# Rotary embedding on one core: the tables are loaded first, the head of batch 0 behind them

## The chip, the cores and the metric

The kernel runs on one core of one Trainium2 chip. Its time is the device time of one execution in microseconds (us). Before the change the median of three runs is 316.88 us (316.84 to 317.36). The core has several engines with an instruction stream each; four of them do something here: VectorE (DVE) multiplies and adds, ScalarE (ACT) converts number formats, and GpSimd (POOL) and SyncE (SP) issue transfers. The transfers are carried out by the core's 16 DMA engines. On-chip memory has 128 partitions.

## The reference: what is computed

```
x1, x2 = x[..., :32], x[..., 32:]        # x: (8, 2048, 16, 64) float32
out1 = x1 * cos - x2 * sin               # cos, sin: (2048, 32) float32
out2 = x1 * sin + x2 * cos               # the same table row for all 8 batches and 16 heads
out  = concatenate([out1, out2], axis=-1)
```

Each batch is 8 MB (2048 x 16 x 64 float32), so 64 MB are read and 64 MB are written; the tables have 256 KB each. Per element there are two products and a sum.

## The kernel before

A batch's 2048 positions are split so that partition p has positions 16p to 16p+15 (J = 16 "rows" in each partition). One tile `xt` holds a whole batch in float16, 128 partitions x 16384 elements; `io_pool` has five such buffers (NBUF = 5). The conversions between float32 in the main memory and float16 on the chip are made in the transfers that GpSimd issues (q0 in the profile): `load` (line 52) and `store` (line 60) are such casting transfers, of one 64 KB row of the main memory for each partition.

All of GpSimd's transfers go through one ring and are worked off in the order in which they were issued. That order is: loads of batches 0 to 3; the first row of batch 0 as a store (line 100, `first`); load 4; the rest of batch 0; batch 1; load 5 (it waits until batch 0's stores have landed, because it takes its buffer); load 6 (waits for batch 1's store); stores 2 and 3; load 7 (waits for store 2); stores 4, 5 and 6; and batch 7 in two parts (lines 130 and 132).

At the start and at the end SyncE's queue (q1) helps, which moves data without a cast. At the start it brings the first two rows of each partition of batch 0 as float32 into the tile `head` (JA = 2, 1 MB, line 36), and ScalarE converts them into `xt` (line 84; line 52's first load leaves these rows out, so it has 14 rows). Behind the head SyncE issues the sine and the cosine table (lines 44 and 45). ScalarE makes three float16 operands of them: the sine, the negative sine (both in `sin_h`, lines 88 and 89) and the cosine (`cos_h`, line 90). At the end ScalarE converts the last two rows of batch 7 into `head` (line 140) and SyncE stores them (line 141) once the part of line 130 has landed.

`rotate` is VectorE's work on a batch: v = (swapped halves of xt) x sin_h (line 73), xt = xt x cos_h (line 79), xt = xt + v (line 81). It is called for the two head rows first, then for the other 14 of batch 0, and then once for each batch.

ScalarE's stream before the change is: activation table, head cast (line 84), the two sine casts, the cosine cast, and much later line 140. Each engine works its stream in order, so a wait holds everything behind it. In the changed file the lines are numbered otherwise: the tables' issues are 40 and 41, the head's is 42, the casts are 84 to 86 for the tables and 87 for the head. From the stores on the numbers are the same in both.

Of the kernel before, what the change touches and what calls it, by code (L numbers as in the profile page):

```python
# [1 line left out]

# [4 lines left out]


@with_exitstack  # L10
def kernel(
    ctx: ExitStack,
    tc: tile.TileContext,
    x: bass.AP,
    cos: bass.AP,
    sin: bass.AP,
    out: bass.AP,
):
    nc = tc.nc
    f16 = mybir.dt.float16  # L20
    f32 = mybir.dt.float32

    B, S, H, D = x.shape
    Dh = D // 2
    P = nc.NUM_PARTITIONS
    J = S // P
    NBUF = 5

    const_pool = ctx.enter_context(tc.tile_pool(name="rope_const", bufs=1))
    io_pool = ctx.enter_context(tc.tile_pool(name="rope_io", bufs=NBUF))  # L30
    tmp_pool = ctx.enter_context(tc.tile_pool(name="rope_tmp", bufs=1))

    JA = 2
    head = const_pool.tile([P, JA, H, D], f32)
    x0 = x[0].rearrange("(p j) h d -> p j (h d)", j=J)
    nc.sync.dma_start(  # L36
        out=head.rearrange("p j h d -> p (j h d)"),
        in_=x0[:, 0:JA, :].rearrange("p j f -> p (j f)"),
    )
    sin_f = const_pool.tile([P, J, Dh], f32)  # L40
    cos_f = const_pool.tile([P, J, Dh], f32)
    cos_h = const_pool.tile([P, J, Dh], f16)
    sin_h = const_pool.tile([P, J, D], f16)
    nc.sync.dma_start(out=sin_f, in_=sin.rearrange("(p j) d -> p j d", j=J))  # L44
    nc.sync.dma_start(out=cos_f, in_=cos.rearrange("(p j) d -> p j d", j=J))

    loads = []

    def load(b):
        xt = io_pool.tile([P, J, H, D], f16)  # L50
        j0 = JA if b == 0 else 0
        dma = nc.gpsimd.dma_start(  # L52
            out=xt[:, j0:J, :, :].rearrange("p j h d -> p (j h d)"),
            in_=x[b].rearrange("(p j) h d -> p j (h d)", j=J)[:, j0:J, :].rearrange("p j f -> p (j f)"),
        )
        loads.append(dma)
        return xt

    def store(b, xt, j0=0):
        return nc.gpsimd.dma_start(  # L60
            out=out[b].rearrange("(p j) h d -> p j (h d)", j=J)[:, j0:J, :].rearrange("p j f -> p (j f)"),
            in_=xt[:, j0:J, :, :].rearrange("p j h d -> p (j h d)"),
        )

    def rotate(xt, j0, j1):
        v = tmp_pool.tile([P, J, H, D], f16)
        n = j1 - j0
        js = slice(j0, j1)
        shape = [P, n, H, 2, Dh]
        sin_b = sin_h[:, js, :].rearrange("p j (e d) -> p j e d", e=2).unsqueeze(2).to_broadcast(shape)  # L70
        cos_b = cos_h[:, js, :].unsqueeze(2).to_broadcast([P, n, 2 * H, Dh])
        xe = xt[:, js, :, :].rearrange("p j h (e d) -> p j h e d", e=2)
        nc.vector.tensor_mul(  # L73
            out=v[:, js, :, :].rearrange("p j h (e d) -> p j h e d", e=2),
            in0=xe[:, :, :, ::-1, :],
            in1=sin_b,
        )
        xw = xt[:, js, :, :].rearrange("p j h (e d) -> p j (h e) d", d=Dh)
        nc.vector.tensor_mul(out=xw, in0=xw, in1=cos_b)  # L79
        xa = xt[:, js, :, :].rearrange("p j h d -> p (j h d)")  # L80
        nc.vector.tensor_add(out=xa, in0=xa, in1=v[:, js, :, :].rearrange("p j h d -> p (j h d)"))  # L81

    tiles = [load(b) for b in range(NBUF - 1)]
    nc.scalar.copy(  # L84
        out=tiles[0][:, 0:JA, :, :].rearrange("p j h d -> p (j h d)"),
        in_=head.rearrange("p j h d -> p (j h d)"),
    )
    nc.scalar.copy(out=sin_h[:, :, Dh:D], in_=sin_f)  # L88
    nc.scalar.mul(out=sin_h[:, :, 0:Dh], in_=sin_f, mul=-1.0)  # L89
    nc.scalar.copy(out=cos_h, in_=cos_f)  # L90
    rotate(tiles[0], 0, JA)
    def part(b, j0, j1):
        return (
            out[b].rearrange("(p j) h d -> p j (h d)", j=J)[:, j0:j1, :].rearrange("p j f -> p (j f)"),
            tiles[b][:, j0:j1, :, :].rearrange("p j h d -> p (j h d)"),
        )

    def store_rows(b, j0, j1):
        dst, src = part(b, j0, j1)
        return nc.gpsimd.dma_start(out=dst, in_=src)  # L100

    first = store_rows(0, 0, 1)
    tc.add_manual_dep(
        first.ins,
        loads[NBUF - 2].ins.name,
        mybir.DependencyInfo(mybir.DependencyClass.NoSync, mybir.DependencyReason.DATA),
        reason="order of the ring",
    )
    tiles.append(load(NBUF - 1))
    tc.add_manual_dep(  # L110
        loads[NBUF - 1].ins,
        first.ins.name,
        mybir.DependencyInfo(mybir.DependencyClass.NoSync, mybir.DependencyReason.DATA),
        reason="order of the ring",
    )
    for b in range(B):
        rotate(tiles[b], JA if b == 0 else 0, J)
        if b < B - 1:
            st = store(b, tiles[b], 1 if b == 0 else 0)
            if b == 0:  # L120
                tc.add_manual_dep(
                    st.ins,
                    first.ins.name,
                    mybir.DependencyInfo(mybir.DependencyClass.NoSync, mybir.DependencyReason.DATA),
                    reason="order of the ring",
                )
        if b + NBUF < B:
            tiles.append(load(b + NBUF))
    dst, src = part(B - 1, 0, 9)
    gate = nc.gpsimd.dma_start(out=dst, in_=src)  # L130
    dst, src = part(B - 1, 9, J - JA)
    rest = nc.gpsimd.dma_start(out=dst, in_=src)  # L132
    tc.add_manual_dep(
        rest.ins,
        gate.ins.name,
        mybir.DependencyInfo(mybir.DependencyClass.NoSync, mybir.DependencyReason.DATA),
        reason="order of the ring",
    )
    dst, src = part(B - 1, J - JA, J)
    nc.scalar.copy(out=head.rearrange("p j h d -> p (j h d)"), in_=src)  # L140
    end = nc.sync.dma_start(out=dst, in_=head.rearrange("p j h d -> p (j h d)"))
    tc.add_manual_dep(
        end.ins,
        gate.ins.name,
        mybir.DependencyInfo(mybir.DependencyClass.Sync, mybir.DependencyReason.DATA),
        reason="the last rows go out behind this part",
    )


# [1 line left out]
_INS = ['x', 'cos', 'sin']  # L151
_OUTS = [((8, 2048, 16, 64), 'float32')]


# [23 lines left out]
```

## Time and profile before

| what | us |
|---|---|
| median of 3 runs | 316.88 (316.84 to 317.36) |
| span of the profiled execution | 315.7 |
| VectorE busy | 209.1 |
| ScalarE busy | 6.8 |
| GpSimd busy (it issues transfers) | 9.9 |
| first product on VectorE starts / third of them ends | 15.86 / 36.78 |
| first store issued | 37.06 |
| load of batch 7 issued / landed | 199.17 / 237.44 |
| last store issued | 306.43 |

The profiled execution is one execution recorded by the hardware; its span runs from the first to the last instruction, and the page gives no other time of it. The time of a run has some 1.2 us around such a span. In the profile "x3" is a count, "L73" a line of the kernel, "v<-xt,sin_h" an operation by its operands, and an arrow in the list of waits says whom an engine waited for. Rows of the list of waits give the total, how many times, and the longest. A DMA share of 1.00 means that all 16 DMA engines had a packet under way all the time. The table of transfer issues gives the size and the median time from the issue to the landing. "Landing" is the moment when all parts of a transfer have been signalled.

### The profile page before, as it was taken

The numbers are of one execution on the slowest core, as the hardware profiler recorded it, in microseconds if no ns is written. First come the engines' busy times: TensorE is split into PE (matmuls) and PEld (weight loads), VectorE is DVE, ScalarE is ACT, GpSimd is POOL, SyncE is SP. The second block draws the span as 40 slices with busy tenths as digits, with TensorE's granted clock in tenths as the row PEclk, the third lists the DMA queues.
The fourth block names the chain that finished last, engine by engine and source line by source line (L and its number), as shares of the span: only waits on it lengthen the run. The fifth ranks groups of instructions, "written<-read, shape, count | busy, mean of one in ns | idle before, by whom it ended". The sixth has DMA issues, their size and how long they took to land.

```text
span 315.7 us, 122 instructions
## 1 busy us (share of the span) xinstructions
DVE 209.1 (66%) x27; ACT 6.8 (2%) x6; POOL 9.9 (3%) x22
## 2 busy tenths in 40 slices
DVE  0010699999999999999999999994009994000000
ACT  4100000000000000000000000000000002000000
POOL 3000100000000000001000000100000001000000
DMA  9899999999999989999999999999999999999998
GB/s 277 183 262 208 199 220 245 199 199 199 266 199 199 498 374 523 399 332 241 224 199 199 390 407 399 399 531 266 199 249 482 399 399 515 415 399 399 432 434 330
DMA packets 3168, 101.71 MB, mean 322 GB/s; under 512 B 352, under 2 KB 352, under 8 KB 736
## 3 DMA queue, kind: packets, MB, share of 16 engines
q0 software_dynamic: 2592, 99.09, 98.1%
q1 hardware_dynamic: 576, 2.62, 2.3%
HBM read 67.63 MB, written 67.11 MB: 427 GB/s over the span
## 4 chain that ended last, share of the span: by engine, by line
DVE 25%; DMA 22%; issue 18%; another core or an unknown queue 17%; POOL 1%; ACT 1%; SPq 0%; POOLq 0%; DVEq 0%; ACTq 0%
DMA xt<-in_x_dram 12%; DMA cos_f<-in_cos_dram 10%; DVE xt L79 8%; DVE xt L81 8%; DVE v L73 8%; ACT head L140 1%; POOL out_dram L60 1%; POOL xt L52 0%; ACT cos_h L90 0%; SPq L44 0%; SPq L36 0%; POOLq L52 0%; POOLq L60 0%; DVEq L73 0%
## 5 line engine op out<-in xcount | busy, mean ns | idle before, releaser
L73 DVE TENSOR_TENSOR v<-xt,sin_h 128x16384 f16<-128x16384 f16 (+2 forms) x9 | 69.7, 7744 | 36.8 <-DMA xt<-in_x_dram 20.7
L79 DVE TENSOR_TENSOR xt<-xt,cos_h 128x16384 f16<-128x16384 f16 (+2 forms) x9 | 69.7, 7744 | 17.5 <-ACT cos_h L90 17.2
L81 DVE TENSOR_TENSOR xt<-xt,v 128x16384 f16<-128x16384 f16 (+2 forms) x9 | 69.7, 7744 | 0.3
L52 POOL DMA_DIRECT2D xt<-in_x_dram x8 | 4.4, 557 | 111.1 <-DMA out_dram<-xt 110.3
L140 ACT CAST head<-xt 128x2048 f32<-128x2048 f16 x1 | 1.9, 1897 | 229.5 <-DVE xt L81 229.5
L60 POOL DMA_DIRECT2D out_dram<-xt x7 | 3.7, 535 | 63.9 <-DVE xt L81 63.9
L130 POOL DMA_DIRECT2D out_dram<-xt x1 | 0.5, 531 | 46.3 <-DVE xt L81 46.3
L84 ACT CAST xt<-head 128x2048 f16<-128x2048 f32 x1 | 1.9, 1897 | 3.6 <-DMA head<-in_x_dram 3.6
L100 POOL DMA_DIRECT2D out_dram<-xt x1 | 0.5, 541 | 33.5 <-DVE xt L81 33.5
L84 ACT ACT_TABLE_LOAD x1 | 1.3, 1283 | 0.7 <-PEq L162 0.7
L90 ACT CAST cos_h<-cos_f 128x512 f16<-128x512 f32 x1 | 0.6, 618 | 17.8 <-DMA cos_f<-in_cos_dram 17.8
L88 ACT CAST sin_h<-sin_f 128x512 f16<-128x512 f32 x1 | 0.6, 617 | 7.2 <-DMA sin_f<-in_sin_dram 7.2
L89 ACT ACTIVATE sin_h<-sin_f 128x512 f16<-128x512 f32 x1 | 0.6, 624 | 0.0
L132 POOL DMA_DIRECT2D out_dram<-xt x1 | 0.5, 531 | 0.0
L162 POOL MEMSET const-float32-0.0<- 128x1 f32 x1 | 0.1, 99 | 0.2 <-issue 0.2
L162 POOL MEMSET const-bfloat16-1.0<- 128x1 bf16 x1 | 0.1, 102 | 0.0
L162 POOL MEMSET const-float32-1.0<- 128x1 f32 x1 | 0.1, 99 | 0.0
L162 POOL MEMSET const-uint8-127<- 128x1 uint8 x1 | 0.1, 99 | 0.0
## 6 DMA issues: line engine op xcount, KB each, us to landing
xt<-in_x_dram POOLq DMA_DIRECT2D x7, 4096.0 KB, 41.3
out_dram<-xt POOLq DMA_DIRECT2D x1, 7680.0 KB, 61.6
out_dram<-xt POOLq DMA_DIRECT2D x1, 4608.0 KB, 42.4
xt<-in_x_dram POOLq DMA_DIRECT2D x1, 3584.0 KB, 22.3
out_dram<-xt POOLq DMA_DIRECT2D x1, 2560.0 KB, 47.9
head<-in_x_dram SPq DMA_DIRECT2D x1, 1024.0 KB, 4.8
out_dram<-head SPq DMA_DIRECT2D x1, 1024.0 KB, 8.4
out_dram<-xt POOLq DMA_DIRECT2D x1, 512.0 KB, 47.1
```

The lines of the kernel that those rows point to most:

```text
L52: dma = nc.gpsimd.dma_start(out=xt[:, j0:J, :, :].rearrange("p j h d -> p (j h d)"), in_=x[b].rearrange("(p j) h d -> p j (h d)", j=J)[:, ...
L60: return nc.gpsimd.dma_start(out=out[b].rearrange("(p j) h d -> p j (h d)", j=J)[:, j0:J, :].rearrange("p j f -> p (j f)"), in_=xt[:, j0:J ...
L73: nc.vector.tensor_mul(out=v[:, js, :, :].rearrange("p j h (e d) -> p j h e d", e=2), in0=xe[:, :, :, ::-1, :], in1=sin_b,)
L79: nc.vector.tensor_mul(out=xw, in0=xw, in1=cos_b)
L81: nc.vector.tensor_add(out=xa, in0=xa, in1=v[:, js, :, :].rearrange("p j h d -> p (j h d)"))
L84: nc.scalar.copy(out=tiles[0][:, 0:JA, :, :].rearrange("p j h d -> p (j h d)"), in_=head.rearrange("p j h d -> p (j h d)"),)
L88: nc.scalar.copy(out=sin_h[:, :, Dh:D], in_=sin_f)
L89: nc.scalar.mul(out=sin_h[:, :, 0:Dh], in_=sin_f, mul=-1.0)
L90: nc.scalar.copy(out=cos_h, in_=cos_f)
L100: return nc.gpsimd.dma_start(out=dst, in_=src)
L130: gate = nc.gpsimd.dma_start(out=dst, in_=src)
L140: nc.scalar.copy(out=head.rearrange("p j h d -> p (j h d)"), in_=src)
```

## The change

SyncE asks for the sine and the cosine table first and for the head behind them, where the head was first. ScalarE's four conversions are put into the same order: three for the tables, then the head. Nothing else is edited; the streams of VectorE and GpSimd have the same instructions in the same order.

```diff
     head = const_pool.tile([P, JA, H, D], f32)
     x0 = x[0].rearrange("(p j) h d -> p j (h d)", j=J)
-    nc.sync.dma_start(
-        out=head.rearrange("p j h d -> p (j h d)"),
-        in_=x0[:, 0:JA, :].rearrange("p j f -> p (j f)"),
-    )
     sin_f = const_pool.tile([P, J, Dh], f32)
     cos_f = const_pool.tile([P, J, Dh], f32)
     cos_h = const_pool.tile([P, J, Dh], f16)
     sin_h = const_pool.tile([P, J, D], f16)
     nc.sync.dma_start(out=sin_f, in_=sin.rearrange("(p j) d -> p j d", j=J))
     nc.sync.dma_start(out=cos_f, in_=cos.rearrange("(p j) d -> p j d", j=J))
+    nc.sync.dma_start(
+        out=head.rearrange("p j h d -> p (j h d)"),
+        in_=x0[:, 0:JA, :].rearrange("p j f -> p (j f)"),
+    )
...
     tiles = [load(b) for b in range(NBUF - 1)]
+    nc.scalar.copy(out=sin_h[:, :, Dh:D], in_=sin_f)
+    nc.scalar.mul(out=sin_h[:, :, 0:Dh], in_=sin_f, mul=-1.0)
+    nc.scalar.copy(out=cos_h, in_=cos_f)
     nc.scalar.copy(
         out=tiles[0][:, 0:JA, :, :].rearrange("p j h d -> p (j h d)"),
         in_=head.rearrange("p j h d -> p (j h d)"),
     )
-    nc.scalar.copy(out=sin_h[:, :, Dh:D], in_=sin_f)
-    nc.scalar.mul(out=sin_h[:, :, 0:Dh], in_=sin_f, mul=-1.0)
-    nc.scalar.copy(out=cos_h, in_=cos_f)
     rotate(tiles[0], 0, JA)
```

## The prediction

> **What bounds the kernel now.** I read the page's head and its DMA row first, then the queues' shares, then the work by stretches, and last the waits and the issue times that could turn the order of the ring.
>
> ```profile
> span 315.7 us, 122 instructions
> DVE 209.1 (66%) x27; ACT 6.8 (2%) x6; POOL 9.9 (3%) x22
> DMA  9899999999999989999999999999999999999998
> q0 software_dynamic: 2592, 99.09, 98.1%
> q1 hardware_dynamic: 576, 2.62, 2.3%
> ```
>
> VectorE works 66% of the span, the 16 DMA engines all of it: GpSimd's queue (q0) alone fills 98.1%, SyncE's (q1) adds 2.3%. The sum is over 100% because records of neighbouring packets overlap a little. By stretches (columns: stretch, its length, busy DVE, ACT, POOL with counts, clock, DMA share, GB/s):
>
> ```profile
> 0.00:1.70 1.70, 0.00 (x0) 0.96 (x1) 0.65 (x5) 1.00 0.00 0
> 1.70:5.20 3.50, 0.00 (x0) 0.32 (x1) 1.81 (x4) 1.00 0.97 329
> 5.20:37.00 31.80, 3.87 (x4) 3.66 (x4) 0.00 (x0) 1.00 1.03 228
> 37.00:86.00 49.00, 48.80 (x7) 0.00 (x0) 1.61 (x3) 1.00 1.03 221
> ...
> 264.00:306.00 42.00, 0.00 (x0) 1.67 (x1) 1.02 (x2) 1.00 0.99 420
> 306.00:315.70 9.70, 0.00 (x0) 0.00 (x0) 0.00 (x0) 1.00 0.84 345
> ```
>
> Nothing moves for 1.7 us, then the DMA share is 0.97 to 1.03 until the last stretch. In the trace's packet records I put packets end to end into 16 streams: no real gap between the first packet (1.73) and the last (314.5). A 64 KB row of GpSimd's queue takes 2.43 us whatever VectorE does. So the end is: first packet, plus the sum of all packets. VectorE, in 5.2:37, is idle for 28 of 32 us and it costs nothing so long as the ring stays filled. That is what the chain of waits hides; it hangs its start on the cosine table. The waits that matter:
>
> ```profile
> DVE v L73 <- DMA xt<-in_x_dram: 20.7, 1, 20.7
> ACT cos_h L90 <- DMA cos_f<-in_cos_dram: 17.8, 1, 17.8
> DVE xt L79 <- ACT cos_h L90: 17.2, 1, 17.2
> DVE v L73 <- ACT sin_h L89: 15.9, 1, 15.9
> ```
>
> The last three (the change is aimed at them) lie before 36 us. The first, 20.7 us, is VectorE waiting for the load of batch 7 at 237.5, which was issued at 199.17 when a store landed: a time set by the ring. Whatever VectorE gains early it waits out there or at a load before.
>
> **The change part by part.** The sum is made against the profiled execution: span 315.7; the median 316.88 stands 1.2 us above it, and I carry those 1.2 us over unchanged.
>
> 1. SyncE's three issues. Removed from the front: head (0.37 us of issue); put there: sine and cosine (0.42 each). All three still go out between 0.74 and 2.05, none waits; what stands behind them on SyncE is the last store, which waits 304.3 us. The head is issued at about 1.6 instead of 0.74: 0.84 us later. First packet 1.0 us after the first issue, as before (1.73). Cost 0: no instruction's issue time is on the path, only that packets are always there.
>
> 2. What moves before GpSimd's loads flow.
>
> ```profile
> head<-in_x_dram SPq DMA_DIRECT2D x1, 1024.0 KB, 4.8
> sin_f<-in_sin_dram SPq DMA_DIRECT2D x1, 256.0 KB, 13.5
> cos_f<-in_cos_dram SPq DMA_DIRECT2D x1, 256.0 KB, 32.0
> out_dram<-head SPq DMA_DIRECT2D x1, 1024.0 KB, 8.4
> ```
>
> Each engine holds 8 rows of each (8 KB of the head, 2 KB of a table). The packet records show 309 ns for a head row and 84 ns for a table row alone, 96 ns for a table row between load rows. The first load packet starts at 5.28, on every engine after 8 head rows and about 6 sine rows; from then on the queues alternate, one small row per load row, which is why 256 KB of cosine need 32.0 us. After the change the tables stand in the free part and the head, or most of it, in the alternating part. Bytes are the same. Ten table rows per engine get 12 ns cheaper (-0.12 us); eight head rows get dearer: by 12 ns like a table row (+0.10), or by the 33 ns that the last store's 8 KB rows show beside GpSimd's rows (342 against 309: +0.26). Net -0.02 to +0.14. A cruder price from the queue's records by window: 0:5.2 moved 1.15 MB in 65.1% of 5.2 us, 2.94 us per MB; 306:315.7 moved 1.05 MB interleaved in 25.9% of 9.7 us, 2.39 us per MB: 1.05 MB moved from the one to the other would save 0.6. That first price has the cold start of the first packets in it, which stays whoever is first, so I take +0.05 and keep -0.6 as an end.
>
> 3. The cold start with 2 KB rows. No row of before shows tables as the first packets. The head's first rows took 0.6 to 1.3 us instead of 0.31. If a table's first packets start likewise, sine is through at 1.73 + 0.6 + 8 x 0.084 = 3.0, cosine (issued 0.42 later, there at about 2.2) at 3.7, and the head is there at 2.7: no gap, cost 0. If the start-up part were paid again for the second and third transfer, 2 x 0.6 = +1.2. In the trace the sine rows follow the head's on each engine without a gap, nearest to the case, so 0. Lower end 0: the first 1.7 us are not touched.
>
> The Trainium skill ("DMA: Bandwidth & Descriptors", section Bandwidth and the fit in its anatomy of one DMA) speaks against small transfers in front: batch to 1 MiB or more, each DMA having some 2.0 us fixed. Were the engines idle for two such fixed parts, the sum would be 316.9 + 4.0 = 320.9. The 1.15 MB that three transfers moved by 5.2 us do not look so, since fixed parts lay under each other.
>
> 4. ScalarE: three casts (0.62 us each) go ahead of one of 1.90. Same instructions. It now waits for sine, cosine, then head; behind the head's cast only the cast of L140 waits, at 263.8.
>
> 5. VectorE and the ring. Its first product now waits for the head's cast. If the switch to alternation comes after 14 small rows again, the loads start at 1.9 (the mean engine's first packet) + 0.6 + 14 x 0.084 = 3.7; 2 cosine rows, 8 head rows and 2 completion marks follow in 12 turns, as many as before (2 sine, 8 cosine, 2 marks: 5.3 to 33.6, 28.3 us), and the eight rows in them are 0.23 us longer each. The head lands at 3.7 + 28.3 + 1.8, about 34, its cast ends at 36, three small products (1.24 each) end at 39.8 against 36.8: VectorE 3 us later. If the loads become ready at 5.3 regardless, five head rows are through by then, four turns remain, the head lands near 15 and VectorE is through at 21: 16 us earlier. I lean to the first (all engines switched at the same count) but the time does not hang on it. Who waits: the first store (L100) at 37.06, and behind it on POOL the fifth load. The four loads ahead fill the ring to about 82.9 (last issue 3.0 + 79.9), so the first store has 45 us to spare; the rest of batch 0 is issued at 60.04 and is needed when the fifth load lands (37.6 + 65.9 = 103.5): 43; batch 1, issued 86.22, is needed at 121.6: 35. Later issues wait for landings. 3 us late or 16 early lies under that cover: 0. With the cover gone, each us late past 35 would cost one.
>
> Sum: 0 + 0.05 + 0 + 0 + 0; 316.9.
>
> **The rivals.**
> *A. The start gets gaps (slower).* Place: 1.7 to 5.2 us. Mechanism: cosine's and head's first packets don't overlap the transfer ahead, 2 x 0.6 us: 318.1 (+0.4%). It decides from one exposed 0.63 us on. For it: the head's slow first packets, 2 KB rows are never first before. Against: sine behind head without a gap, and load rows fill in once they are ready.
> *B. VectorE's start reaches the end (faster).* Were VectorE the bound, up to 16 us: 301. For it: the chain of waits begins with the cosine. Against: the 20.7 us wait at 237.5 and the full DMA row.
> *C. The interleaved head is truly cheaper.* 2.39 instead of 2.94 us per MB: 316.3. Against: the first price holds the cold start.
> *D. The change doesn't do what it says:* the head takes the cosine's place as the late one, VectorE starts no earlier. It is the first case of 5, gives 316.9, and is in the forecast.
>
> **How the numbers follow.** The runs before spread over 0.52 us, and 0.2% (0.63 us) is about what a measurement can tell from no change. Within 0.2%: 0.79 (my sum and D). A with smaller costs of the same kind: 0.13. C 0.06 and B 0.02, together faster 0.08. The range takes C's 316.3 at the low end and most of A, one start-up part and the spread of runs, at the high end: 317.8.
>
> **What the profile after would show.** The DMA row full from the first slice, q0 near 98%; the share in 1.7:5.2 still about 0.97 (A: below 0.8); sine and cosine landing within 4 us of issue (head within 34, or about 14 in the second case); VectorE's first product after the head's cast; its wait for batch 7 again 17 to 22 us (3 us late shortens it; more than a little early it waits already for batch 5, whose load, issued at 122.19 and some 41 us under way, sets 164); the last store issued near 306.4. Wrong would be a first store issued after 80, or a gap in the DMA row.

## The result, and the profile after

The change makes the kernel slower by 0.42%: ratio 1.0042 (95% interval 1.0029 to 1.0056), 21 executions of each. The ratio lies near that of the means (318.26 us against 316.96 us); the medians, 318.57 us against 316.88 us, are 0.53% apart. Either one hides the shape. The executions of before lie in one group (316.52 to 317.51). Those of after lie in two: 6 from 316.63 to 317.16, and 15 from 318.23 to 319.50, with nothing between. The profiled execution is of the upper group (318.81 us, 1.8 us above its span). In all runs whose span stands beside the time, the two are 1.7 to 1.8 us apart, not the 1.2 us that the part on the profile before took. So the profiled execution of before, with its span of 315.7, took about 317.45 us, some 0.55 us above its median: the two pages differ by 1.3 us in span, the two groups of after by 2.0 us. From here on "upper" means above 318.0.

The page of after, and its answer on the same stretches (stretch, length, busy DVE, ACT, POOL with counts, clock, DMA share, GB/s):

```profile
span 317.0 us, 121 instructions
DVE 209.1 (66%) x27; ACT 6.7 (2%) x6; POOL 9.9 (3%) x22
DMA  8999999999999999999999999999999999999996
q0 software_dynamic: 2592, 99.09, 97.7%
q1 hardware_dynamic: 576, 2.62, 2.1%
```

```profile
0.00:1.70 1.70, 0.00 (x0) 0.96 (x1) 0.65 (x5) 1.00 0.00 0
1.70:5.20 3.50, 0.00 (x0) 1.95 (x4) 1.81 (x4) 1.00 1.11 281
5.20:37.00 31.80, 8.51 (x4) 1.92 (x2) 1.07 (x2) 1.00 1.01 230
...
306.00:317.00 11.00, 0.00 (x0) 0.00 (x0) 0.00 (x0) 1.00 0.76 313
```

The DMA row still looks full. The first digit is 8 where it was 9, and the last is 6 where it was 8: something is missing at both ends. The share of 1.7:5.2 says 1.11, more than before, and misleads: a record counts where it begins, and load rows of more than 2 us begin in this stretch now. The GB/s beside it, 281 against 329, point the other way, with the same caution. Spread over their own durations, the packet records fill 0.95 of this stretch before and 0.78 after; at 4.2 us, 16 records are under way before and 12 after.

The waits and the issues (size, then us from issue to landing):

```profile
DVE v L73 <- ACT xt L87: 28.4, 1, 28.4
DVE v L73 <- DMA xt<-in_x_dram: 26.8, 2, 24.9
ACT xt L87 <- DMA head<-in_x_dram: 21.2, 1, 21.2
```

```profile
head<-in_x_dram SPq DMA_DIRECT2D x1, 1024.0 KB, 24.8
...
sin_f<-in_sin_dram SPq DMA_DIRECT2D x1, 256.0 KB, 2.8
cos_f<-in_cos_dram SPq DMA_DIRECT2D x1, 256.0 KB, 2.9
```

The tables land 2.8 and 2.9 us after their issue, the head 24.8. VectorE starts its first product at 28.39 and its third one ends at 32.14, 4.6 us earlier than before; it waits 24.9 us for batch 7 where it waited 20.7. So VectorE's gain was waited out, and the time went elsewhere.

It went on the DMA engines, and the end shows it. The DMA row of the stretch 314 to 316, in slices of 0.05 us, first of before, then of after:

```profile
DMA  9004000000000000000000000000000000000000
```

```profile
DMA  0303730033730033330033303030303000000000
```

Here too a record counts where it begins: a digit of 3 is one row of the last store that begins in that slice (0.31 us out of 16 x 0.05 us), a 7 is two. Before, the last row begins at 314.2 and is over at 314.5. After, rows begin until 315.5 and the last is over at 315.8. Counted by their durations, five records are under way from 314.4 to 314.8, four at 315.0, three at 315.4: five of the 16 engines are still at work while the others are done. At the start there are five late ones as well. These are the first load rows of the 16 engines, start in us / duration in ns, in order of start:

```
before: 5.28 to 5.68, all 2129
after:  3.52/2489 3.52/2411 3.53/2172 3.54/2256 3.55/2505 3.56/2222 3.58/2199 3.60/2240
        3.68/2129 3.69/2129 3.79/2129 3.92/2959 4.61/2688 4.76/2975 4.88/2704 5.18/2419
```

With the tables alone in front, the loads begin at 3.5 instead of 5.3. Five engines get their first row 0.4 to 1.7 us after the first one, and it takes up to 2.98 us instead of 2.13. These five rows end at 6.9 to 7.7, the eleven others at 5.7 to 6.1; at the far end five engines finish at 314.9 to 315.8, eleven by 314.3. The records carry no engine number, so that they are the same five is read from the number and the size of the lateness. The other engines, idle by then, do not take rows off the late ones, and the last store, which waits for a transfer's landing on all of them, is issued at 307.8 instead of 306.4.

### The profile page after: what moved, and what is told of

Its sections match the earlier page's. It is cut to its first block, busy times and chain, and to the rows that moved or that the text cites. A ratio compares the mean times of both kernels' runs of the same rounds, so it can differ in the third digit from the quotient of the medians.

```text
span 317.0 us, 121 instructions
## 1 busy us (share of the span) xinstructions
DVE 209.1 (66%) x27; ACT 6.7 (2%) x6; POOL 9.9 (3%) x22
## 3 DMA queue, kind: packets, MB, share of 16 engines
q1 hardware_dynamic: 576, 2.62, 2.1%
## 4 chain that ended last, share of the span: by engine, by line
DVE 25%; DMA 20%; another core or an unknown queue 19%; issue 18%; ACT 1%; POOL 1%; SPq 0%; POOLq 0%; DVEq 0%; ACTq 0%
DMA xt<-in_x_dram 12%; DVE xt L81 8%; DVE v L73 8%; DVE xt L79 8%; DMA head<-in_x_dram 8%; ACT xt L87 1%; ACT head L140 1%; POOL out_dram L60 1%; POOL xt L52 0%; SPq L41 0%; SPq L40 0%; POOLq L52 0%; POOLq L60 0%; DVEq L73 0%
## 6 DMA issues: line engine op xcount, KB each, us to landing
head<-in_x_dram SPq DMA_DIRECT2D x1, 1024.0 KB, 24.8
```

## The experiments

Theory S: the change shortens what stands ahead of GpSimd's loads, and engines then lose time at their first load row. Its first rival V: the order on ScalarE and VectorE costs the time. The later rivals are about why the rows are late. "Two groups" is read as the share of upper executions; of the kernel before, 3 of 129 executions over all comparisons were above 318.0.

**SyncE's order alone (e1).** After with ScalarE's lines put back:

```diff
+    nc.scalar.copy(out=tiles[0][:, 0:JA, ...], in_=head...)
     nc.scalar.copy(out=sin_h[:, :, Dh:D], in_=sin_f)
...
-    nc.scalar.copy(out=tiles[0][:, 0:JA, ...], in_=head...)
```

> SyncE's new order alone; ScalarE's lines are left as before. Theory S (the short cover): eight sine and eight cosine rows of 2 KB are worked off by 3.7 us instead of 5.3, GpSimd's loads follow at once, and some of the 16 DMA engines stand idle before their first load row and stay late to the end: 318 to 319.5, as with the whole change, with some executions near 316.8. Rival V (ScalarE's and VectorE's order costs the time): 316.9.

Measured: 316.88 median, 7 executions from 316.55 to 316.92 and 5 from 318.91 to 319.18; ratio 1.0016 (0.9994 to 1.0038). The instruction streams of this kernel turned out to be those of the whole change: ScalarE's stream is ordered when the program is built, and it puts the tables first whatever the lines say. So this is the changed kernel again, and the ratio differs from 1.0042 by how many executions fell into the upper group (5 of 12 against 15 of 21). Its profiled execution was of the lower group: span 315.1, first load rows from 3.49 to 3.86 with none late, 2.13 to 2.39 us each, and in the stretch 314 to 316 nothing moves any more:

```profile
DMA  0000000000000000000000000000000000000000
```

**ScalarE's order alone (e2).** Before, with a dependency that holds the head's cast behind the cosine's:

```diff
-    nc.scalar.copy(out=tiles[0][:, 0:JA, ...], in_=head...)
+    c1 = nc.scalar.copy(out=tiles[0][:, 0:JA, ...], in_=head...)
...
+    tc.add_manual_dep(c1.ins, c2.ins.name, NoSync, ...)   # c2: the cast into cos_h
```

> ScalarE's new order alone (forced by a dependency of the head's cast on the cosine's), SyncE as before. Theory S: the head's cast then waits for the cosine at 33.6, VectorE's first product moves from 15.9 to about 36.2 and its third ends at 39.9 instead of 36.8, 3 us later, and the time stays at 316.9 (within 0.3). Rival V: 318 or more.

Measured: 317.21, ratio 1.0002 (0.9993 to 1.0011), no upper execution. VectorE starts at 35.94 instead of 15.86, the third small product ends 3 us later than before, and its wait for batch 7 shrinks by 3.4 us, from 20.7 to:

```profile
DVE v L73 <- ACT xt L84: 35.9, 1, 35.9
...
DVE v L73 <- DMA xt<-in_x_dram: 17.3, 1, 17.3
```

V is out: a late VectorE costs nothing here. As e1 is the whole change, this run is also what leaves SyncE's order as the part that costs the time.

**The head from another batch (e4).** Before, with x[B - 1] in place of x[0] as the head's source.

> SyncE's order as before, but the head's 1 MB is read from batch 7 instead of batch 0 (two of batch 0's 16 rows come out wrong). Rival C (the first reads of a stretch of x are slow, and before the change the head paid that for batch 0's rows): the first load rows become slow and late on some engines, 318 or more. Theory S: 16 rows of the same sizes stand ahead of the loads, the first load row starts at 5.3 without a gap, 316.9.

Measured: 317.07, ratio 0.9998 (0.9988 to 1.0008), one of 11 at 318.02. The first load rows start from 5.13, 14 of 16 within 5.51, one at 6.04. No two groups: rows of batch 0 need not have been read by the head. It says nothing about a stretch as large as all of x.

**A pause of GpSimd behind load 0 (p2).**

```diff
+        if b == 1:
+            nc.gpsimd.memset(xt[:, J - 4 : J, :, :]..., 0.0)
         dma = nc.gpsimd.dma_start(
```

> The changed kernel, but GpSimd fills 4096 elements of the second tile with zeros between its first and its second load, so that for some 2 to 4 us it writes no descriptors of loads 1 to 3. If the engines are held up because GpSimd is still writing the descriptors of loads 1 to 3 while the first load's are fetched (D1), the gaps go: 316.9 and a first load row of 2.13 us everywhere. If the hold-up lies in the reads themselves (S with slow first reads) or in the descriptors of load 0 alone, it stays: 318 to 319.

Measured: 317.54, ratio 1.0020 (0.9997 to 1.0043); 7 lower, 5 upper (318.73 to 319.68). The pause was 3.5 us (loads 1 to 3 are issued from 5.75 on), and in the profiled execution, an upper one, two engines begin at 5.29 and 5.83, the other 14 by 3.97. D1 is out as the cause of the late rows.

**The head between the tables (e3).** SyncE: sine, head, cosine.

> SyncE asks for sine, head, cosine; ScalarE follows that order. If the switch to GpSimd's loads comes by count (some 14 to 16 rows of SyncE's queue first), eight small and six large rows stand ahead of the loads: the first load row starts at about 4.6 us, between 3.6 (both tables ahead) and 5.3 (head ahead). Theory S (length of cover): fewer late executions than with the tables first, where 20 of 33 were above 317.9; median 316.9 to 317.3. Theory T (it is the cold start with 2 KB rows that does it): as with the tables first.

Measured: 316.82, ratio 0.9997 (0.9989 to 1.0006), no upper execution among 11. The first load rows start at 5.27 to 5.63, not 4.6: the loads wait for all 16 rows of the first two transfers. Theory T in its form "2 KB rows first" falls; S stands for now.

**The loads later (p1).**

```diff
+        if b == 0:
+            nc.gpsimd.memset(xt[:, J - 2 : J, :, :]..., 0.0)
         dma = nc.gpsimd.dma_start(
```

> The changed kernel, but GpSimd first fills 2048 elements of the first tile with zeros (about 1.8 us), so the loads are issued from about 3.1 us on; the tables and most of the head's large rows can go ahead of them until about 5.4. D2 (a fixed lateness between GpSimd's issue of a load and its descriptors being there on each engine, during which the engine stands): the gaps move with the issue and stay as long, executions at 318 to 319.5 as often as with the change. S with slow first reads behind small rows (R): the first load row starts at 5.4 behind large rows without a gap, nearly all executions at 316.5 to 317.5.

Measured: 319.37, ratio 1.0071 (1.0058 to 1.0084), all five executions from 318.60 up. Neither expectation is met, and this run taught most. The loads are issued from 2.85 on, so head rows follow the tables, from 3.43 on. Five head rows begun between 3.88 and 4.90 take 1.19 to 1.66 us instead of 0.31, before any load row has begun. So a row of SyncE's queue can be late too, without a load row ahead of it or beside it (GpSimd is issuing the loads meanwhile, from 2.85 to 5.11). The stretch 3.6 to 5.2 in SyncE's queue (packets, MB, share), first of this run, then of e3, both with head rows under way:

```profile
q1 hardware_dynamic: 67, 0.47, 92.5%
```

```profile
q1 hardware_dynamic: 84, 0.69, 102.5%
```

With 16 table rows ahead 0.47 MB move, with 8 ahead 0.69. The load rows then start anywhere from 6.0 to 9.1, and 13 of the first 16 take over 2.2 us.

**SyncE's queue later (p3).** After, with 24 fills of sin_f on VectorE that the first transfer has to wait for.

> The changed kernel, but VectorE fills sin_f 24 times first, which SyncE's first transfer has to wait for, so GpSimd's loads start on empty engines. It shows when load rows can start by themselves. If they are ready by about 2.5 to 3.6 on all engines and full speed from the first row, neither descriptors nor reads are slow by themselves, and the lateness needs SyncE's small rows in front; the time is 316.9 plus the later first packet (some 1 to 2 us), in one group. If some engines start up to 5.3, the lateness belongs to the loads' own start: two groups 2 us apart, 318 to 320.5.

Measured: 336.32, ratio 1.0611 (1.0597 to 1.0625), far from what was expected: the tables' and the head's rows alternated with load rows, and the head landed so late that VectorE's first product began at 84.88 and its third ended at 88.64, when the ring had run dry. That is the price of step 5's cover: third product 51.9 us later than before, less 35 us of cover, gives 316.9 + 16.9 = 333.8; measured 336.3. The run also shows load rows on idle engines: they start at 2.62 to 3.32, 1.4 to 2.1 us after the issue, and all take longer than 2.13 (2.33 to 3.08). So the first large rows are slow by themselves, but none was over 0.7 us later than the first. The DMA row of the whole span falls to 5 and 6 tenths between 75 and 92 us and again at 125 to 142, as nowhere in before:

```profile
DMA  8989999996588895589898898989898989899997
```

**A small transfer in front (p8, x1, x2).** After, with one more transfer ahead of the sine: 64 bytes for each partition, from batch 0 of x (p8), the sine table (x1) or batch 7 of x (x2).

```diff
+    touch = const_pool.tile([P, 16], f32)
+    nc.sync.dma_start(out=touch, in_=x[0]...[:, JA * H * D : JA * H * D + 16])
     nc.sync.dma_start(out=sin_f, in_=sin.rearrange("(p j) d -> p j d", j=J))
```

> The changed kernel with one small transfer more ahead of the sine: 64 bytes of each partition's first load row. If the first touch of these stretches of x is what is slow (C2), the touch takes it over and the load rows behind start at full speed: nearly all at 316.6 to 317. If not, the two groups stay: some at 316.7, more than a third at 318 to 319.5.

> The run with the touch again, same shape and place, but its 64 bytes per partition come from the sine table, not from x. C2 (the first read of x, when it comes behind the tables, is what holds engines up): the upper group is back, a third or more at 318.5 to 320. C3 (one small transfer more, or the 0.4 us by which it shifts the rest, does it, whatever it reads): one group at 317.3 to 317.7, as with the touch of x.

> The touch reads batch 7 of x instead of batch 0. C2 with stretches as large as the tensor: one group at 317.3 to 317.7, as with the touch of batch 0. C2 with small stretches (a batch or less): the upper group is back, a third or more at 318.5 to 320. C3: one group.

Measured: p8 317.48 (317.32 to 317.68), x1 317.50 (317.06 to 318.13), x2 317.34 (317.03 to 317.73), 11 executions each, ratios 1.0015 (1.0006 to 1.0023), 1.0001 (0.9991 to 1.0010), 0.9996 (0.9988 to 1.0005). One group each, one execution of the 33 above 318.0. The control x1 decides: what the small transfer reads does not matter, so the first touch of x (C2) is out. In these runs the loads begin at 3.2, behind 8 small and 8 sine rows; the cosine then alternates with them. All first load rows are somewhat slow (x1: 2.13 to 2.92 us), none is over 0.7 us late. The loads begin earlier here than after the change (3.5) and yet there is no upper group, so a short cover by itself, theory S as it was stated, is not the cause either.

**The changed kernel once more (r1), and the tables' tiles filled from x (x3).**

> The changed kernel once more, to compare the next three with it on one chip. Every theory: two groups of executions, near 316.7 and near 318.9, with a third to three quarters in the upper one.

> The changed kernel with the same transfers in the same order and shape, but the two table tiles are filled from rows of batch 0 of x, 2 KB for each partition (the output is then not the rotation). C2: x is touched at 1.7 us, nothing holds the load rows up, one group at 316.6 to 317.2. T (2 KB rows ahead of the loads, whatever they read): two groups 2 us apart, as with the change.

Measured on the chip of x1 and x2: r1 318.72, 5 lower (one of them at 317.90) and 7 upper, ratio 1.0024 (1.0006 to 1.0042). x3 319.19, ratio 1.0056 (1.0043 to 1.0069), all five upper: reading x early with 16 rows of 2 KB does not help. (Its 2 KB rows are 64 KB apart in memory, the tables' rows lie side by side; by itself it would not settle C2.) Over after, e1 and r1, one program, 27 of 45 executions are upper.

**No head (x4), the head only when the tables are in (x5), the cosine through ScalarE's queue (x6).**

```diff
 # x4: the head's transfer and cast are gone, load 0 has all 16 rows
-        j0 = JA if b == 0 else 0
+        j0 = 0
 # x5
+    tc.add_manual_dep(d3.ins, d2.ins.name, Sync, ...)   # d3: head, d2: cosine
 # x6
-    nc.sync.dma_start(out=cos_f, in_=cos.rearrange("(p j) d -> p j d", j=J))
+    nc.scalar.dma_start(out=cos_f, in_=cos.rearrange("(p j) d -> p j d", j=J))
```

> The changed kernel without the head: the tables first, and GpSimd's first load brings all 16 rows of batch 0. If the load rows are held up by what the 16 table rows ahead of them did (T), two groups stay, near 316.8 and near 319. If the head as SyncE's third transfer, its rows mixed with the first load rows, is needed for it (H), one group at 316.6 to 317.2.

> The changed kernel, but SyncE issues the head only when the cosine table has landed (at about 4.5 instead of 1.63), so no head row can stand beside the first load rows at 3.5 to 5. H: one group at 316.6 to 317.2, which would be the fastest form seen. T: two groups, near 316.8 and near 319.

> The changed kernel with the cosine table issued by ScalarE's own queue beside the sine, and the head second on SyncE's: all three asked for by 1.6 us. H as the third place in SyncE's queue: the upper group goes, 316.6 to 317.2. If it is only the head's rows beside the first load rows, whichever place they have in a queue, or the 16 table rows, the upper group stays at 318.5 to 319.5 in a third or more.

Measured: x4 319.25 (all five from 319.08 to 319.39), ratio 1.0076 (1.0064 to 1.0088); x5 318.83, 4 lower and 8 upper, ratio 1.0046 (1.0029 to 1.0063); x6 316.88 (316.71 to 317.16, 11 executions), ratio 1.0001 (0.9992 to 1.0010). The head is not needed for the loss (x4), and asking for it later does not help (x5): H is out; T in the form "16 rows of 2 KB of one queue, then large rows" is what all runs leave standing (x3 shows that the rows need not be the tables'). In x6 the tables come from two queues, the head's rows follow at 3.6 at 0.31 us each, and the loads start at 5.4 to 5.8, all at 2.13 us. The Trainium skill ("DMA: Bandwidth & Descriptors", section Issuing engines are not separate DMA queues) says that spreading transfers over issuing engines saves issue time only. x6 shows one thing more: with the cosine on a second queue the upper group of after is gone. But the head is then SyncE's second transfer, as in e3, which loses the upper group without a second queue; that the second queue itself does it is not shown.

**What the profiles of the two groups have in common.** Five upper profiles begin their loads behind 16 rows of 2 KB: after, p2, x3, x4 and x5. The number of clearly late first load rows in them is 5, 2, 2, 2 and 2, and as many records are still under way near the end (at 314.8 us in after, at 315.0 in the others). In each of them the last first load row starts 1.5 to 2.3 us behind the first, in the lower profiles of the same program (e1, r1) 0.4 to 0.5 us, and there the last packet is over by 313.9. This ties the 2 us to the late rows.

**What stays open.** Large rows (the loads', or p1's head rows) that come directly behind 16 rows of 2 KB of SyncE's queue are late on two to five engines in the upper profiles, and 27 of 45 executions of the changed program are upper; behind 16 rows of which 8 were the head's, or 8 only 64 bytes, or 8 came through another queue (x6, whose head rows follow the 2 KB rows directly), they are not. Why the memory or the engines do that was not found. The p3 run shows that the first large rows on idle engines are slow; that 16 engines ask for them in the same instant while small rows have not yet brought the reading up to speed is a guess, not shown.

## Why the prediction was wrong

- **What bounds the kernel:** right. The DMA engines bound it, and the time is the sum of the packets plus gaps. I took it for granted that all engines end together; it is the slowest of 16 engines that sets the end, and here they end up to 1.8 us apart (eleven by about 314.0 to 314.3, the last at 315.8). The 1.2 us that I carried over from the span to the time are 1.7 to 1.8 in every run; the forecast of 316.9 does not suffer, since it starts from the median.
- **Step 1 (SyncE's issues):** right; sine at 0.74, cosine at 1.15, head at 1.63, first packet at 1.75.
- **Step 2 (dearer and cheaper rows):** right in size. Head rows between load rows take 322 ns where I put 321 to 342. The lower group of after (middle value 316.8) lies where before does (316.88), so the 0.6 us of rival C did not show.
- **Step 3 (the cold start with 2 KB rows, "so 0"):** this step failed. The tables themselves were through by 3.8, near the 3.7 that I had worked out, and two more fixed parts (320.9) were not paid; the 2.0 us that I took for them from the Trainium skill ("DMA: Bandwidth & Descriptors", section Anatomy of one DMA) are a fit for transfers that GpSimd issues, and these were SyncE's. But the step asked only whether the packets of SyncE's queue would follow each other, and took the loads behind them for ready at full speed, because in before every first load row took 2.13 us. There it came behind 3.5 us of reading, 1 MB of it in 8 KB rows. Behind the tables it is late on some engines, a cost that the sum had at 0: 2.0 us between the two groups of after (middle values 316.8 and 318.8), and 27 of 45 executions in the upper one. Why large rows are late there stays open.
- **Rival A** named this place and sign, priced 1.2 us (318.1) and given 0.13 together with its like. The place was right (1.7 to 5.2), the mechanism was not: the tables pay no start-up part a second and third time, and the gaps lie between the last table row and the first load row of some engines. That its 1.2 us are near the 1.3 us between the means is luck, since the groups are 2.0 us apart. The sign it tells by (share under 0.8 in 1.7:5.2) did not come in the view, which says 1.11 because records count where they begin; spread over their durations they give 0.78, so the sign was there. The upper group reaches 319.5, and the range ended at 317.8.
- **Step 4 (ScalarE):** right; e2 shows it by itself, and e1 that the edit's second half changes nothing in the program that the first half doesn't.
- **Step 5 (VectorE and the ring):** the outcome was right, 0. Both my cases for the head's landing (34 and 15) were off; it was 26.4. The switch came after all 16 table rows, not after 14, so nine or ten turns with load rows remained instead of 12. The size of the cover (35 us) held in p3 to within 2.5 us of the time.
- **Rival B** fell as said: VectorE 4.6 us earlier, wait for batch 7 up by 4.2 us.

## What to carry to other kernels

In a kernel that the DMA engines bound, the first microseconds matter less for when the data are there than for whether all 16 engines get going together: here no engine took rows off a late one, and the engines that started up to 1.7 us late ended up to 1.8 us late after 310 us of work. A large transfer among the first two of SyncE's queue was such a start here; two small ones of 2 KB rows were not, though they hand the consumer its tables 10 and 30 us sooner. A median that moves by 0.5% can be two groups 2 us apart: look at the single times before explaining it, and get a profile of each group.

## What the runs showed of the hardware that I had not expected

- With the loads issued at 1.25, each DMA engine first served some 16 rows of SyncE's queue (two transfers; about 14 in before), whatever their size, then took turns with GpSimd's, one row each. The loads began at 3.2 (64 B and 2 KB rows), 3.5 (2 KB), 5.3 (8 KB and 2 KB). So what stood ahead of the loads was set by rows, not by bytes or time, as long as the loads were issued that early (in p1, issued at 2.85, they began at 6.0). The Trainium skill ("DMA: Bandwidth & Descriptors", section Queues, rings and completion order) has an engine drain a packet of some 9 to 17 descriptors before it changes queue; the 16 at the start, two transfers of 8 rows, lie in that range; the one-to-one turns later do not.
- Load rows that meet idle engines are slow at first (p3: 2.33 to 3.08 us against 2.13), the head's first 8 KB rows likewise (0.46 to 1.27 against 0.31 in before). In p8, x1 and x2, where all engines pay some of it, the medians are 0.5, 0.05 and -0.1 us from those of before.
- No version tried is faster than the kernel before, clear of the noise: sine, head, cosine (0.9997) and the cosine on ScalarE's queue (1.0001) equal it, though VectorE starts at 10.05 instead of 15.86 in the first of them. Eleven of the 16 other runs have their fastest execution at 316.5 to 317.1; that this is the floor that 16 full engines set is a guess.
